# Two-layer hybrid encoder trunk: the two sequences as one token block, or as two streams half a layer apart

## The chip, the core and the metric

The kernel runs on one core of one Trainium2 chip. Its engines are TensorE (PE; PEld is its weight load), VectorE (DVE), ScalarE (ACT), GpSimd (POOL) and SyncE (SP), which issues nearly all DMAs. Each engine takes its instructions in a fixed order. The metric is the device time of one execution in microseconds, smaller being better.

## The reference, cut to what matters

A trunk of two layers runs over two independent sequences, a prompt of 512 tokens and a sample of 256, each with 16 learned meta tokens ahead: 528 and 272 tokens, 800 together. All weights are shared by both.

```python
for l in range(DEPTH):                                   # 2 layers, D = 1024
    proj = rms_norm(h, norm_mix[l]) @ w_in[l]            # 1024 x 2944
    xa, ga, xq, xi, xff, xfb, xg, xu = split(proj)
    ya = rglru_branch(xa, ga, ...)                       # 384 wide, scans in both directions
    yb = hgrn2_branch(xq, xi, xff, xfb, xg, ...)         # 384 wide, chunks of 64 tokens
    yc = s5_branch(xu, ...)                              # 256 wide, 16 groups of 16 with 64 complex states
    ym = concat([rms_norm(ya), rms_norm(yb), rms_norm(yc)]) * mix_gain[l]
    h = h + ym @ w_out[l]                                # 1024 x 1024
    h = h + relu(rms_norm(h, norm_mlp[l]) @ w_up[l])**2 @ w_down[l]   # 4096 wide
return rms_norm(h[:, N_META:], norm_final)
y_prompt, y_sample = _trunk(x_prompt, ...), _trunk(x_sample, ...)
```

## The kernel before

Features lie on partitions and the 800 tokens of both sequences along the free dimension. A product (`product`, L426) multiplies blocks of 128 x 128 weights with two halves of 400 tokens each and gathers over k in one PSUM bank; there are three such banks ("mm"). Weights and operands are float32, split exactly into a float32r high part and a low part, and three passes are made: high by high (L434), high weight by low operand (L435), low weight by high operand (L436). In layer 1 the meta tokens fall away after the mixers: w_out runs over 512 + 256 tokens there and the MLP over 384 + 384.

A block of weights is 128 columns of 1024 rows, 512 KB. `fetch` (L441) issues its DMA into one of three buffers "wr"; `wsplit` (L416) makes the high part with a ScalarE copy (L419) and the low part with a GpSimd subtraction (L420), two buffers each. Each weight is read once. An activation's result u in the MLP is split in the same way (L1128 ScalarE, L1129 GpSimd); relu and square are L1123 and L1124, and w_down's products are added to the residual by L1150.

The mixers of a layer (`mix`, L985) are issued as steps by a hand-written list per layer, `ORDERS`: `hi`/`hc`/`gh`/`hf` are the projections, chain, gate and end of an HGRN tile (chain `hgrn`, L597 to L694), `ri`/`rc` an RG-LRU tile, `si`/`sc`/`sf` the S5 projection, scan (`s5`, L879, eight groups per 128 features with table loads "E", "F", "TB", "W") and gated end. `PR` moves some steps in priority, `TG`, `NB` and `MO` say where they take their SBUF, and `KS` which outputs stay on chip; the others go to DRAM (`keep`, L1019) and come back (`finish`, L1001). `fA`, `fB`, `fC` normalise a group and split it into w_out's operands. `mix_out` (L1066) runs w_out in three passes in layer 0 and two in layer 1, a pass for the groups that are done (`LT`); a late group is scaled by the tokens' 1/rms after its product (L1098, L1099). The S5 tables (a step size, decays, their powers) are made by `s5_setup` (L706 to L872), whose DVE arithmetic is L726 to L731: for layer 0 at the start, for layer 1 within the first MLP, behind a mark in its first w_down. The order on each engine follows from issue order and priorities.

Of the kernel before, what the change touches and what calls it, by code (L numbers as in the profile page):

```python
# [30 lines left out]
SEQ = ((0, 528), (528, 272))
T = 800
EPS = 1e-6
NCH = 100
XA, GA, XQ, XI, XFF, XFB, XG, XU = 0, 384, 768, 1152, 1536, 1920, 2304, 2688
CH = [16 + 64 * n for n in range(8)] + [544 + 64 * n for n in range(4)]
# [38 lines left out]

class Trunk:
    def __init__(self, ctx, tc, ins, outs):
# [1157 lines left out]
```

## Time and profile before

| | |
|---|---|
| median of 3 runs (lowest, highest) | 2200.86 us (2199.04, 2205.67) |
| the profiled execution, its span | 2201.6 us (the page gives no other time of it) |
| busy: PE, DVE, ACT, POOL | 2087.4, 1118.9, 753.8, 811.9 us |
| instructions of PE, DVE, ACT, POOL | 14,082, 2,258, 1,141, 622 |
| DMA | 160.74 MB, 73 GB/s on average |
| queue of SP's DMAs, share of 16 engines' span | 23.8% |

Busy time is a sum over the span; an engine that is busy for 37% can still set the end of a stage. The stages of the span are, in order: start, setup and layer-0 mixers (to about 565 us), layer-0 w_out and MLP (to 1165), layer-1 mixers with w_out (to 1635), layer-1 MLP (to 2185), and the store-out. A row of the trace gives an instruction's start and duration, its engine, line and operands and, in brackets, how long the engine had been idle before it and what ended that.

### The profile page before, as it was taken

To read this page: it belongs to the slowest core of one execution; us is meant where nothing else is said; L and a number is where in the kernel's file an instruction comes from. 1 tells how busy PE (TensorE), PEld (TensorE's weight loads), DVE (VectorE), ACT (ScalarE), POOL (GpSimd) and SP (SyncE) were. 2 spreads that over 40 slices of the span, in tenths; PEclk is the share of its full clock that TensorE was granted. 3 is DMA by queue.
4 is the path that set the end of the run, shared out by engine and by line. 5 is a ranking of instruction groups with operands and counts; after the bars stand their busy time and mean duration, and the time that the engine had idled before them with its cause. 6 is when DMAs were issued, how large, how long until landed. Compare 5 with 4: busy or idle time off the path is not lost.

```text
span 2201.6 us, 34495 instructions
## 1 busy us (share of the span) xinstructions
PE 2087.4 (95%) x14082; PEld 1957.7 (89%) x14082; DVE 1118.9 (51%) x2258; ACT 753.8 (34%) x1141; POOL 811.9 (37%) x622
## 2 busy tenths in 40 slices
PE   8899899889989899999999999998998999999998
PEld 6889897677979899999998879886888999999997
DVE  6884748487657871221155855746368221112224
ACT  6233535454322232212225553436432122222222
POOL 1672112263433443333444213322434343434343
PEclk9899899899999999999999999998999999999998
DMA  5322111342211431122122113221321112122221
GB/s 182 96 81 76 38 40 56 101 129 57 68 48 58 109 119 58 58 64 61 58 95 78 57 37 97 74 59 48 113 79 58 58 58 68 59 67 65 60 67 68
DMA packets 230886, 160.74 MB, mean 73 GB/s; under 512 B 33270, under 2 KB 217784, under 8 KB 230728
## 3 DMA queue, kind: packets, MB, share of 16 engines
q1 hardware_dynamic: 229832, 156.95, 23.8%
q8 instruction: 111, 1.82, 0.4%
q10 hardware_dynamic: 896, 1.58, 0.2%
q14 instruction: 47, 0.39, 0.1%
HBM read 131.32 MB, written 27.18 MB: 72 GB/s over the span
## 4 chain that ended last, share of the span: by engine, by line
PE 60%; DVE 10%; ACT 2%; issue 1%; POOL 1%; DMA 1%; SPq 0%; DVEq 0%; POOLq 0%; ACTq 0%
PE mm L435 18%; PE mm L434 18%; PE mm L436 18%; PE hb L664 2%; PE hb L582 1%; DVE m L1163 1%; DVE h L1172 1%; PE rb L510 1%; DVE xl L379 1%; DVE m L1164 1%; DVE h L1154 1%; DVE r L1173 0%; DVE m L1124 0%; PE rb L862 0%; POOL wl L420 0%
## 5 line engine op out<-in xcount | busy, mean ns | idle before, releaser
L420 POOL TENSOR_TENSOR wl<-wr,wh 128x1024 fp32r<-128x1024 f32 (+3 forms) x214 | 479.3, 2240 | 1005.5 <-ACT wh L419 982.7
L434 PE MATMUL mm<-xh,wh 128*128 128x400 f32 (+3 forms) x2016 | 710.2, 354 | 33.1 <-DVE m L1124 11.1
L435 PE MATMUL mm<-xl,wh 128*128 128x400 f32 (+3 forms) x2016 | 713.9, 355 | 6.0 <-POOL xl L383 2.9
L436 PE MATMUL mm<-xh,wl 128*128 128x400 f32 (+3 forms) x2016 | 701.1, 349 | 0.7 <-POOL wl L420 0.5
L419 ACT ACTIVATE wh<-wr 128x1024 fp32r<-128x1024 f32 (+3 forms) x214 | 205.7, 962 | 764.9 <-PE mm L435 658.5
L434 PEld LDWEIGHTS mm<-xh,wh 128*128 128x128 f32 x2016 | 388.6, 193 | 52.7 <-DVE m L1124 14.1
L435 PEld LDWEIGHTS mm<-xl,wh 128*128 128x128 f32 x2016 | 389.1, 193 | 18.5 <-DVE xl L379 4.1
L436 PEld LDWEIGHTS mm<-xh,wl 128*128 128x128 f32 x2016 | 388.8, 193 | 8.9 <-POOL wl L420 0.9
L434 PE MATMUL mm<-u,wh 128*128 128x400 f32 (+1 forms) x1024 | 349.1, 341 | 6.2 <-DVE m L1124 6.2
L435 PE MATMUL mm<-u,wh 128*128 128x400 f32 (+1 forms) x1024 | 349.6, 341 | 0.0
L436 PE MATMUL mm<-u,wl 128*128 128x400 f32 (+1 forms) x1024 | 348.3, 340 | 0.0
L1150 DVE TENSOR_TENSOR h<-mm,h 128x400 f32<-128x400 f32 (+1 forms) x256 | 144.5, 565 | 331.2 <-PE mm L436 331.2
L1124 DVE TENSOR_TENSOR m<-m,mm 128x400 f32<-128x400 f32 (+1 forms) x128 | 71.1, 559 | 369.2 <-ACT m L1123 369.2
L434 PEld LDWEIGHTS mm<-u,wh 128*128 128x128 f32 x1024 | 193.3, 189 | 7.8 <-DVE m L1124 7.1
L435 PEld LDWEIGHTS mm<-u,wh 128*128 128x128 f32 x1024 | 193.2, 189 | 0.1
L436 PEld LDWEIGHTS mm<-u,wl 128*128 128x128 f32 x1024 | 193.1, 189 | 0.1
L1129 POOL TENSOR_TENSOR u<-m,u 128x800 fp32r<-128x800 f32 (+1 forms) x64 | 127.3, 1990 | 53.5 <-ACT u L1128 45.4
L1123 ACT ACTIVATE m<-mm 128x400 f32<-128x400 f32 (+1 forms) x128 | 62.3, 489 | 129.9 <-PE mm L436 115.8
L582 PE MATMUL hb<-hs,hs 64*64 64x64 f32 x2016 | 85.7, 236 | 8.8 <-ACT hs L615 5.6
L582 PEld LDWEIGHTS hb<-hs,hs 64*64 64x64 f32 x2016 | 72.2, 146 | 24.5 <-issue 11.4
L1128 ACT ACTIVATE u<-m 128x800 fp32r<-128x800 f32 (+1 forms) x64 | 55.1, 861 | 83.1 <-DVE m L1124 73.2
L616 DVE TENSOR_TENSOR hd<-hd,hd 128x800 f32<-128x800 f32 (+2 forms) x48 | 43.1, 902 | 13.3 <-ACT hs L614 12.8
(365 smaller groups left out, 2245.8 us busy)
## 6 DMA issues: line engine op xcount, KB each, us to landing
wr<-in_w_up_dram SPq DMA_DIRECT2D x64, 512.0 KB
wr<-in_w_down_dram SPq DMA_DIRECT2D x64, 512.0 KB
wr<-in_w_in_dram SPq DMA_DIRECT2D x46, 512.0 KB
h<-h SPq DMA_DIRECT2D x16, 400.0 KB
wr<-in_w_out_dram SPq DMA_DIRECT2D x32, 192.0 KB
TB<-t SPq DMA_DIRECT2D x24, 200.0 KB
F<-t SPq DMA_DIRECT2D x16, 256.0 KB
E<-t SPq DMA_DIRECT2D x16, 256.0 KB
```

What stands on the lines that cost most here:

```text
L419: self.nc.scalar.activation(hi[:], raw, AF.Copy)
L420: self.nc.gpsimd.tensor_tensor(out=lo[:], in0=raw, in1=hi[:].bitcast(F32), op=SUB)
L434: nc.tensor.matmul(ps[:, 0:n], wh, xh[:, c0 : c0 + n], start=(k == 0), stop=False)
L435: nc.tensor.matmul(ps[:, 0:n], wh, xl[:, c0 : c0 + n], start=False, stop=False)
L436: nc.tensor.matmul(ps[:, 0:n], wl, xh[:, c0 : c0 + n], start=False, stop=(k == last))
L582: nc.tensor.matmul(ps[c % 2 * 64 : c % 2 * 64 + 64, c // 2 * 64 : c // 2 * 64 + 64], K[hr, c0 : c0 + 64], Q[hr, c0 : c0 + 64], start=True, ...
L664: mm = lambda out, w, x: nc.tensor.matmul(out, w, x, start=False, stop=False, skip_group_check=True)
L1123: nc.scalar.activation(t[:, sl], ps, AF.Relu)
L1124: nc.vector.tensor_tensor(out=t[:, sl], in0=t[:, sl], in1=ps, op=MULT)
L1128: nc.scalar.activation(u[:, 0], t[:], AF.Copy)
L1129: nc.gpsimd.tensor_tensor(out=u[:, 1], in0=t[:], in1=u[:, 0].bitcast(F32), op=SUB)
L1150: mark = nc.vector.tensor_tensor(out=t[:, sl], in0=ps, in1=t[:, sl], op=ADD)
```

## The change

The class `Trunk` becomes a class `Shared` (constants, parameters, PSUM) and two `Stream`s, a for the prompt (528 tokens, pieces of 272 and 256) and b for the sample (272 tokens, one piece), each with its own SBUF side, its own residual and weight buffers (three wr, two wh and wl each). Each stream reads and splits all weights for itself. In layer 1, w_out and the MLP run over 256 + 256 and 256 tokens. `ORDERS`, `PR`, `TG`, `KS`, `LT` give way to one list for both layers and streams; every mixer output goes to DRAM and returns in `finish`, which scales it ahead of the split; w_out is one pass over eight k tiles after `fC`. S5 uses 66 and 34 chunks of 8 tokens, its scan reads the decay from a column (`r8`) in place of a table. The setup of layer 1 is issued between b's first `feed` and b's second mixers, in a's SBUF.

```diff
-SEQ = ((0, 528), (528, 272))
-ORDERS = [
-    "hi0 hc0 ri0 gr0 hi1 si0 rc0 gr2 hc1 ri1 gh1 hi2 rc1 sc0 hc2 si1 ri2 hf1 hf2 hf0 rc2 fB fA sc1 sf fC",
-    "ri0 rc0 hi0 hc0 ri1 rc1 ri2 rc2 si0 sc0 si1 sc1 sf gh2 hi1 hc1 hi2 gh1 hc2 gr0 hf2 hf0 fA hf1 fC fB",
-]
-HALVES = ((0, 400, 0), (400, 400, 400))
-HALVES_LAST = ((16, 512, 0), (544, 256, 512))
+ORDER = "hi0 hc0 ri0 rc0 gh0 hf0 hi1 hc1 ri1 rc1 gh1 hf1 hi2 hc2 ri2 rc2 gh2 hf2 si0 sc0 si1 sc1 sf fA fB fC"
...
-        def keep(k, y):
-            if k in last:
-                got["y", k] = y
-            else:
-                nc.sync.dma_start(self.ydr[k][:], y[:])
+        keep = lambda k, y: nc.sync.dma_start(self.ydr[k][:], y[:])
...
+        for m in range(KD):
+            raw = self.raw((128, KD, 128))
+            nc.sync.dma_start(raw[:], src[:, :, m * 128 : m * 128 + 128])
+            hi, lo = self.wsplit(raw[:])
+            t, res = self.t("h", (128, n)), self.s((128, n))
+            nc.sync.dma_start(res[:], self.hdr[m][:, self.T - n : self.T])
...
-            if b == 0 and l + 1 < L:
-                with self.using("t", "rb"), self.tc.issue_after(mark.ins):
-                    self.s5_setup(l + 1)
...
+        with a.phase("s0", dict(p=(10752, 1), t=(576, 11)), "t", "rb"):
+            a.setup()
+            a.buffers()
+            b.buffers()
+            with b.phase("i", dict(x=(D, 3), m=(D, 2), h=(b.T, 8)), "m", "rb"):
+                b.load(a)
+            a.s5_setup(0)
+        b.mixers(0, **MIX_B)
+        with a.phase("i", dict(x=(D, 5), m=(D, 1), h=(a.T, 8)), "m", "rb"):
+            a.load(None)
+        a.mixers(0, **MIX_A)
+        b.feed(0, h=8, m=3, u=6)
+        with a.phase("s1", dict(p=(10752, 1), t=(576, 11)), "t", "rb"):
+            a.s5_setup(1)
+        b.mixers(1, **MIX_B)
+        a.feed(0, h=8, m=3, u=6)
+        a.mixers(1, **MIX_A)
+        b.feed(1, h=8, m=3, u=6, t=6)
+        a.feed(1, h=8, m=3, u=6, t=9)
```

`feed` is `mix_out`, `mlp` and the next layer's norm. In the changed kernel the product's passes are L431 to L433, the weight split L416 and L417, the S5 steps L876 to L931 (DVE L896, L897, L906 to L909), relu and square L1052 and L1053, the setup's complex products L700 to L705.

The first place is TensorE's order in layer 0 of the kernel before, while the second half of the S5 runs. Products into "mm" (w_out's first pass, k tile after k tile) stand around the S5 matmuls of a group (L913 input side, L943 output side).

```order
L435 MATMUL mm_787_5143<-xl2_657_4531,wh_783_5126 128x400
L436 MATMUL mm_787_5143<-xh2_656_4530,wl_784_5127 128x400
L434 MATMUL mm_792_5162<-xh0_652_4522,wh_790_5158 128x400
L435 MATMUL mm_792_5162<-xl0_653_4523,wh_790_5158 128x400
L913 MATMUL hb_702_4752<-hs_697_4739 64x100 x8
L434 MATMUL mm_794_5175<-xh0_652_4522,wh_790_5158 128x400
L943 MATMUL hb_695_4723<-hs_689_4683,hs_694_4708 100x128 x4
L943 MATMUL hb_696_4731<-hs_689_4683,hs_694_4708 100x128 x4
L436 MATMUL mm_792_5162<-xh0_652_4522,wl_791_5159 128x400
```

The same place after the change, stream a's S5 in layer 0 (66 chunks): transposes L876, input L893, output L920 and L923.

```order
L923 MATMUL rb_6690<-rs_6651,rs_6677 66x128
L923 MATMUL rb_6698<-rs_6651,rs_6677 66x128
L876 MATMUL rb_6712<-ident_81,rs_6629 128x66 x2
L893 MATMUL rb_6722<-su_6708,rs_6709 64x66 x8
L920 MATMUL rb_6749<-rs_6706,su_6708 66x128
L920 MATMUL rb_6757<-rs_6706,su_6708 66x128
L923 MATMUL rb_6749<-rs_6710,rs_6736 66x128
```

What moved: the products that stood between the S5 matmuls are gone from this stretch (rows 2602 to 2660 of TensorE's order hold none); b's w_out and first w_up blocks stand before it, in the first half of the same S5, and the rest of b's MLP behind it.

The second place is DVE's order. Before, in the layer-0 MLP, where the setup of layer 1 (L726 to L731, tiles t) goes between evacuations of w_up (L1124, from PSUM bank mm):

```order
L726 TENSOR_TENSOR t_1007_6425<-t_1007_6425 128x16
L727 TENSOR_TENSOR t_1007_6425<-t_1007_6425 128x16
L728 TENSOR_TENSOR t_1007_6425<-t_1007_6425 128x16
L1124 TENSOR_TENSOR m_1111_7142<-m_1111_7142,mm_1112_7143 128x400
L730 TENSOR_TENSOR t_1007_6425<-t_1007_6425 128x16
L731 TENSOR_TENSOR t_1007_6425<-t_1007_6425 128x16
```

After, the third evacuation of b's w_up (L1053), row 1014 of DVE's order, with stream a's S5 (L896 to L908) behind it:

```order
L1053 TENSOR_TENSOR m_7436<-m_7436,mm_7437 128x272
L466 SCALAR_TENSOR_TENSOR rs_6552<-rs_6565,rs_6552 128x528
L896 TENSOR_TENSOR rs_6661<-rb_6663,rs_6648 128x264
L897 TENSOR_TENSOR rs_6662<-rb_6663,rs_6648 128x264
L906 SCALAR_TENSOR_TENSOR rs_6676<-r_22_136,rs_6661 128x66 x4
```

And the fourth, row 1307, among the setup of layer 1 (L700 to L705):

```order
L700 TENSOR_TENSOR t_10031<-t_10028,t_9761 128x32
L701 TENSOR_TENSOR t_10031<-t_10027,t_9761 128x32
L704 TENSOR_TENSOR t_9978<-t_9978,t_9982 128x4x2
L1053 TENSOR_TENSOR m_7473<-m_7473,mm_7474 128x272
L705 TENSOR_TENSOR t_9979<-t_9979,t_9982 128x4x2
```

What moved: before, an evacuation stands after some 30 setup instructions all through the setup; now 261 setup instructions and the rest of stream a's S5 and ends stand between the third and the fourth.

## Rows read from the trace of the kernel before

**Rows 1.** The page, busy time of each engine, and the granted clock in 40 slices.

```profile
PE 2087.4 (95%) x14082; PEld 1957.7 (89%) x14082; DVE 1118.9 (51%) x2258; ACT 753.8 (34%) x1141; POOL 811.9 (37%) x622
...
PEclk9899899899999999999999999998999999999998
```

**Rows 2.** Busy time by stretch: window, us, five engines busy, PEclk, DMA share, GB/s.

```profile
0.00:270.00 270.00, 243.01 (x1919) 217.75 (x1920) 200.42 (x589) 116.92 (x193) 112.55 (x132) 0.93 0.33 96
...
565.00:1165.00 600.00, 581.82 (x3164) 573.27 (x3163) 276.30 (x639) 145.32 (x204) 240.45 (x111) 0.98 0.24 73
...
1635.00:2185.00 550.00, 540.96 (x3086) 538.51 (x3085) 159.77 (x236) 127.61 (x166) 221.53 (x100) 0.99 0.20 59
2185.00:2202.00 17.00, 6.39 (x37) 5.70 (x37) 4.56 (x9) 6.12 (x9) 0.00 (x0) 0.59 0.51 186
700.00:750.00 50.00, 41.28 (x200) 39.81 (x199) 48.59 (x216) 8.68 (x12) 21.75 (x17) 0.86 0.39 98
```

**Rows 3.** The page's groups: the high-by-high pass, features and MLP operands.

```profile
L434 PE MATMUL mm<-xh,wh 128*128 128x400 f32 (+3 forms) x2016 | 710.2, 354 | 33.1 <-DVE m L1124 11.1
...
L434 PE MATMUL mm<-u,wh 128*128 128x400 f32 (+1 forms) x1024 | 349.1, 341 | 6.2 <-DVE m L1124 6.2
```

**Rows 4.** Timeline of TensorE, product streams (start us, us, line, operands, columns).

```profile
800.31 0.34 PE L436 MATMUL mm<-xh,wl 128*128 128x400 f32 x1
...
803.04 0.35 PE L436 MATMUL mm<-xh,wl 128*128 128x400 f32 x1
...
1702.52 0.34 PE L436 MATMUL mm<-xh,wl 128*128 128x384 f32 x1
...
1703.04 0.34 PE L436 MATMUL mm<-xh,wl 128*128 128x384 f32 x1
...
1601.90 0.28 PE L435 MATMUL mm<-xl,wh 128*128 128x256 f32 x1
...
1603.45 0.28 PE L436 MATMUL mm<-xh,wl 128*128 128x256 f32 x1
...
1565.79 0.41 PE L435 MATMUL mm<-xl,wh 128*128 128x256 f32 x1
...
1566.43 0.41 PE L435 MATMUL mm<-xl,wh 128*128 128x256 f32 x1
```

**Rows 5.** Splits in the layer-1 MLP by line: count, ns minimum/median/maximum, first and last start.

```profile
L420 POOL TENSOR_TENSOR wl<-wr,wh x36: 2388/2403/2407, 1805.3 to 2098.4; 128x1024 fp32r<-128x1024 f32 x36
...
L419 ACT ACTIVATE wh<-wr x36: 1060/1061/1063, 1804.1 to 2097.3; 128x1024 fp32r<-128x1024 f32 x36
...
L1129 POOL TENSOR_TENSOR u<-m,u x17: 1835/1843/1845, 1824.4 to 2092.3; 128x768 fp32r<-128x768 f32 x17
```

**Rows 6.** Timeline of DVE: start and end of one HGRN tile's chain, layer 1.

```profile
1386.61 1.83 DVE L609 TENSOR_TENSOR hd<-hd,hs 128x1600 f32<-128x1600 f32 x1
...
1472.17 0.99 DVE L693 TENSOR_TENSOR hs<-hs,hs 128x800 f32<-128x800 f32 x1 [5.22 <-ACT hs L413]
```

**Rows 7.** Timeline of DVE: the same step of two successive S5 groups, layer 0.

```profile
483.19 0.57 DVE L915 TENSOR_TENSOR hs<-hb,hs 128x400 f32<-128x400 f32 x1 [1.64 <-POOL hs L935]
...
494.19 0.56 DVE L915 TENSOR_TENSOR hs<-hb,hs 128x400 f32<-128x400 f32 x1
```

**Rows 8.** Timeline: a weight split on POOL, DVE beside it and afterwards.

```profile
798.96 2.40 POOL L420 TENSOR_TENSOR wl<-wr,wh 128x1024 fp32r<-128x1024 f32 x1 [6.94 <-ACT wh L419]
...
799.79 1.89 DVE L728 TENSOR_TENSOR t<-t,t 128x288 f32<-128x288 f32 x1
...
803.69 0.44 DVE L731 TENSOR_TENSOR t<-t,t 128x288 f32<-128x288 f32 x1
```

**Rows 9.** Timeline: a mixer output's store, and first use after its load, layer 1.

```profile
1575.38 0.34 SPq L1019 DMA_DIRECT2D y<-hs  x1
...
1583.03 0.97 ACT L378 ACTIVATE xh<-hs,pc 128x800 fp32r<-128x800 f32 x1 [5.86 <-DMA hs<-y]
```

**Rows 10.** Waits of SP: total us, times, longest, for stores of mixer outputs.

```profile
SPq L1019 <- DVE hs L1046: 21.8, 5, 7.4
```

More of the change, by code (lines that the diff above doesn't have):

```diff
@@ L30 @@
 DIN = 2944
[L31 to L32 removed]
 EPS = 1e-6
[L34 removed]
+NTB = 66
 XA, GA, XQ, XI, XFF, XFB, XG, XU = 0, 384, 768, 1152, 1536, 1920, 2304, 2688
[L36 removed]
 TWO_PI = 2 * math.pi
@@ L284, in load @@
             nc.sync.dma_start(xs[-1][0][:], a)
-            if len(xs) == 4:
+            if len(xs) == 3:
                 self.fetch("w_in", 0, XFF)
-        with self.using("t", "rb"):
-            self.columns(2, [("norm_mix", "l (k p) -> (l k) p")], nc.scalar)
+        if first:
+            first.columns(2, [("norm_mix", "l (k p) -> (l k) p")], nc.scalar)
         gain = self.pc["norm_mix"]
@@ new lines, in hgrn @@
+            prev = None
+            for k in range(n) if d == 0 else range(n - 1, -1, -1):
+                sl = SB[:, d, k]
+                par, at = col[k]
+                new = pss[par][:, at : at + 64]
+                if prev is None:
+                    nc.vector.tensor_copy(sl, new)
+                else:
+                    c = k - (1 - d)
+                    nc.vector.scalar_tensor_tensor(out=sl, in0=prev, scalar=tot[:, d, c : c + 1], in1=new, op0=MULT, op1=ADD)
+                prev = sl
@@ L685, in hgrn @@
+        nc.scalar.activation(O[:, META:T], ps[:, 0 : 64 * n], AF.Copy)
+        nc.scalar.activation(O[:, 0:META], pm[:, mo : mo + META], AF.Copy)
         q = self.s()
         nc.scalar.activation(q[:], O[:], AF.Square)
-        pss = []
-        for b in range(2):
-            ps = self.ps()
-            nc.tensor.matmul(ps[:, 0:400], self.bones[:], q[:, b * 400 : b * 400 + 400], start=True, stop=True)
-            pss.append(ps[:, 0:400])
-        rs = self.rstd(pss, 1.0 / 64, "eps")
+        rs = self.rstd(self.total(q, self.halves, self.bones), 1.0 / 64, "eps")
@@ L946, in s5 @@
-            z = self.s()
-            for b in range(2):
-                ps = self.ps()
-                for j in range(4):
-                    nc.tensor.transpose(ps[:, j * 100 : j * 100 + 100], flat(ZT[b][:, j]), self.ident[0:100, 0:100])
-                nc.scalar.activation(ap(z, b * 4, [[1, 4], [8, 100]]), ps[:, 0:400].rearrange("p (j c) -> p j c", j=4), AF.Copy)
-            self.gelu(z)
+                        nc.tensor.matmul(out, GH[1][r, d, ri], f[d][r, ri], start=False, stop=(d == 1 and ri == 1))
@@ L1060, in mix, with finish @@
-        for w in order:
-            off = PR[l].get(w, 0)
-            self.tc.cur_priority += off
-            step(w)
-            self.tc.cur_priority -= off
+        def finish(k0, nk):
+            ys = []
+            for k in range(k0, k0 + nk):
+                ys.append(self.s())
+                nc.sync.dma_start(ys[-1][:], self.ydr[k][:])
+            r = self.rstd(self.sumsq(ys), 1.0 / (128 * nk), "eps4" if k0 == 3 else "eps16")
+            for k, y in enumerate(ys, k0):
+                self.x[k] = self.split(k, y, self.pc["mix_gain"][:, l * KD + k : l * KD + k + 1], r)
@@ L1066, in mix_out @@
+        for w in ORDER.split():
+            tag = "hs" if w[0] == "h" or w in ("gh0", "gh1", "gh2", "fB") else "ss" if w[0] == "s" and "ss" in self.tags else "rs"
+            with self.using(tag, "hb" if tag == "hs" else "rb"):
+                if w[0] == "f":
+                    finish(*dict(fA=(0, 3), fB=(3, 3), fC=(6, 2))[w])
+                else:
+                    step(w[:2], int(w[2:] or 0))
     def mix_out(self, l):
         nc = self.nc
-        n, halves = (T, HALVES) if l < L - 1 else (768, HALVES_LAST)
@@ new lines, in mix_out, with ev @@
+        for m in range(KD):
[4 more added lines that the diff above has]
+            nc.sync.dma_start(res[:], self.hdr[m][:, self.T - n : self.T])
+            def ev(b, ps, t=t, res=res):
+                c0, w, o = halves[b]
+                nc.vector.tensor_tensor(out=t[:, o : o + w], in0=ps, in1=res[:, o : o + w], op=ADD)
+            self.product([(hi[:, k], lo[:, k]) for k in range(KD)], self.x, halves, ev)
+            new.append(t)
@@ L1106, in mlp @@
         n = h[0].shape[1]
-        halves = HALVES if n == T else ((0, 384, 0), (384, 384, 384))
+        halves = self.halves if n == self.T else tuple((o, w, o) for _, w, o in self.halves_last)
         self.x = [self.split(k, h[k], self.pc["norm_mlp"][:, l * KD + k : l * KD + k + 1], n=n) for k in range(KD)]
@@ new lines, in mixers, with feed @@
+    def mixers(self, l, **k):
+        U = self.T + 3
+        with self.phase(f"m{l}", {t: (dict(gw=512, hm=128, hn=32, su=2 * self.NCH, hd=2 * self.T).get(t, U), n) for t, n in k.items()}, "rs", "rb"):
+            self.mix(l)
+    def feed(self, l, **k):
+        with self.phase(f"f{l}", {t: (dict(u=2 * self.T, t=512).get(t, self.T), n) for t, n in k.items()}, "m", "rb"):
+            h = self.mlp(l, self.mix_out(l))
+            if l + 1 < L:
+                self.norm_in(l + 1, h)
+MIX_A = dict(gw=2, hm=3, hn=4, su=2, hd=5, hs=9, rs=13)
```

723 lines of the change are left out of this document (309 added, 414 removed).

## The prediction

> **What bounds the kernel now.** I read the busy times first [rows 1]: TensorE (PE) works 2087.4 of 2201.6 us and its granted clock is near full all along; the next engine, VectorE (DVE), has half as much. So time is TensorE's work plus the little that it waits, and a stage is slow where its DVE share is high. The table by stage [rows 2] shows it: in the first 270 us DVE is busy for 200.42 us and TensorE idles for 27; in the layer-0 MLP (565 to 1165 us) TensorE works 581.82 of 600 us, in the layer-1 MLP 540.96 of 550. Idle time is 114 us altogether, so the change can win at most that much if it adds no work. The profiled execution (2201.6 us) lies 0.7 us over the median of the runs, 2200.86; the sum below is made against the former, and the difference is ignored.
>
> **The products get shorter, and more of them.** A weight tile of 128 x 128 is used in three passes, which makes 4,560 uses in all (per layer 552 for w_in, 192 for w_out, 768 for w_up, 768 for w_down). Two token halves make 9,120 matmuls now; [rows 3] are two of the groups, six of which make them up. The change has three pieces per pass (272 and 256 columns of the prompt, 272 of the sample), so 13,680. The pace is read from start to start in full streams [rows 4]: at 400 columns 803.04 - 800.31 over 15 steps, 182 ns; at 384 columns 0.52 over 3, 173; at 256 columns 1.55 over 13, 119. For 272 I interpolate: 119 + 16 x (182 - 119)/144 = 126. Per tile and pass 400 + 400 costs 364 ns, 272 + 256 + 272 costs 371: 7.6 ns more with unrounded paces, for 2,832 of those uses (layer 0, and w_in of layer 1). In the layer-1 MLP 384 + 384 becomes 3 x 256: 357 - 346, so 11.6 ns, for 1,536. The 192 of layer-1 w_out (512 + 256 before) I put between, at 8.6. Sum 21.5 + 17.8 + 1.7 = **41 us** of TensorE, all on the path. The Trainium skill, page "TensorE: Matmul & The Clock Gate", section "Back-to-back issue gap", gives an isolated matmul its columns at the full clock and 2.5 ns: 4,560 more would cost 11 us and the forecast would fall by 30; the 182 ns at 400 columns, where that gap would be 169, speak against it here, and the measured paces are taken.
>
> With 24 matmuls to a weight block of 512 KB, the sample (B) uses a block in 24 x 126 ns = 3.03 us (2.86 in layer 1's MLP), the prompt (A) in 24 x 245 = 5.89 (5.72). Without any idle time TensorE would need 2087.4 + 41 = 2128 us, which is a floor.
>
> **The weights are read and split twice.** A split is a ScalarE copy of 1.06 us and a GpSimd subtraction of 2.40 [rows 5]. At 5.89 us per block both hide. At 3.03 they nearly don't: with two buffers, a pair of blocks costs copy, subtraction and one block's matmuls less their start under the end of the split, (1.06 + 2.40 + 3.03 - 0.25)/2 = 3.12 us per block. GpSimd also subtracts the split of u, one of 1.84 us at 768 columns, so 0.65 at 272, per w_up block: 0.33 per block on average. Bounds are 3.03 (all hidden) and 3.8 (copy, subtraction and 0.33 in series); I take 3.12. In the layer-0 MLP the rate of bytes doubles to 172 GB/s; the store-out at the end moved 186 GB/s [rows 2], so it is possible.
>
> **Two streams need two sets of dependent chains.** An HGRN tile's chain of 800 tokens runs 1386.61 to 1472.17 plus 0.99, 86.6 us [rows 6]. The chain of A has 66% of the tokens: 57 if all scales, 86.6 if nothing does; I take 70, the middle, since its many short instructions do not shrink. B (34%): 29 to 86.6, I take 50, nearer the low end since most elementwise work is DVE's. An S5 group of 800 tokens follows the last after 11.0 us [rows 7]; for A 7.3 to 11, taken 9, for B 3.7 to 11, taken 7. In the layer-0 mixers before, w_out's first passes stand between S5 groups (first order fence); now w_out waits for all three groups, and the other stream must give the cover. The second fence says that in A's second S5 half it doesn't: group follows group, no product between. The DVE fences say why: of B's first w_up block only three evacuations have been issued when A's S5 rows come, and the fourth stands behind A's S5 and the second S5 setup (some 261 instructions); three PSUM banks are then full.
>
> Setup on DVE: 216 instructions in 48.59 us (stretch 700 to 750 us) [rows 2], 0.225 each, 59 us for 261; bounds 0 (all beside A's S5) and 88 (1.5 times, by the locked instructions of [rows 8]); I take 59, as nothing else stands between the two evacuations.
>
> **The path, stage by stage (us, running total).**
> - Start to A's first products: DVE has 624 instructions before B's first S5 one: 360 of setup at 0.225 (81) and 264 of the mean 0.34 of the first 270 us (90), 171 at its share of 74% [rows 2] is 230; B's S5, 8 groups x 7 = 56: **286**.
> - A's layer-0 mixers: four blocks before the first chain 24, three chains 210: 520. A's S5 without products 8 x 9 = 72: 592. Setup 59: 651.
> - B's layer-0 w_out and MLP: 72 blocks, of which 14 lie beside A's S5; 58 x 3.12 = 181: 832.
> - Norm 4, B's layer-1 mixers 12 + 3 x 50: 998.
> - A's w_out and MLP, 72 x 5.89 = 424: 1422. A's layer-1 mixers 234: 1656, its S5 72: 1728.
> - B's last MLP 58 x 3.04 = 176: 1904. A's, alone, 72 x 5.72 = 412: 2316. Norm 4 and the tail 17, as now (the last stretch) [rows 2]: 2337, rounded to **2340**.
>
> *Mixer outputs through DRAM.* A store and load takes 1575.38 to 1583.03, 7.7 us [rows 9]. All but the last pair per stream and layer return early; those four would cost 31 us if bare; A's S5 end and B's products stand beside, so I take 0 (ends 0 and 31). SP issues in order, so a store that waits for its data holds the other stream's weights: five such stores held it 21.8 us, 4.4 each, 7.4 at most [rows 10]. There are 32 stores for 9: 23 x 4.4 = 101 as upper end; two blocks in the other buffers cover 6.1 us of products, so 0. *Fewer w_out passes* remove 48 evacuations and 48 additions on DVE, no matmul; DVE is not the limit there: 0. *No decay table*: the scan reads a broadcast column, fewer DMA bytes, 0. *A's load* lies behind B's mixers and only its first operands are awaited: within the start's term.
>
> **The rivals.**
> *R1, the streams do cover each other, not slower.* The order is a queue, not a clock: if B's w_out and w_up fill A's S5 stretches, the 72 + 59 + 72 go: 2340 - 203 = 2137, near the floor. For it: B's blocks are in the list beside A's S5. Against: evacuation four's place behind the setup, a fixed order. It decides from 140 us covered on. 6%.
> *R2, weight supply and split bind B.* At 3.8 us per block, 116 blocks cost 79 more: 2420. For it: GpSimd's 3.05 us of work per w_up block exceed the 3.03 of its matmuls. Against: w_down blocks carry no u. 10%.
> *R3, GpSimd locks out DVE in the mixers.* A DVE multiply of 0.44 us took 1.89 beside a 2.40 us subtraction that was first [rows 8], 1.45 lost. 62 more splits (46 of w_in, 16 of w_out) fall into mixers where DVE sets the end: 90 us, 2430. It decides if the chains, rather than the products, set A's mixer stages. 12%. The Trainium skill, page "SBUF — State Buffer", section "Who interferes with whom", has the rule: a DVE instruction with two SBUF inputs and a GpSimd instruction that reads SBUF exclude each other, the first one holding the port; the trace agrees with it in those 1.89 us.
> The forecast itself, in-order stalls as summed: 72%.
>
> **How the numbers follow.** Ends about the sum: A's chains (6) -77 and +100, B's (3) -62 and +110, setup -59 and +29, splits -10 and +79, S5 of A -27 and +32, of B -26 and +32, trips +31, SP +101. They will not all fall together; as root of the squares 121 below, 206 above. Where TensorE is left thin its clock falls: at the lower level a 256-column matmul takes 213 ns, not 119 (at 1565 us) [rows 4], which lies within the upper ends. Nine tenths below and seven tenths above: **2230 to 2490**. That takes in R2 and R3 and leaves out R1 and the far tail, 20% together. A measurement tells 0.3%, about 7 us, from no change. Faster 0.05 (R1, most of it), same 0.02, slower 0.93.
>
> **What would show it.** Right: TensorE busy above 2128 us by little but idle by some 200; matmuls x13,680 at 0.126 us pace; gaps of TensorE in A's S5 stretches ended by DVE evacuations (L1053) or S5 steps; B's MLP blocks at about 3.1 us, waiting on L416 or L417; A's last MLP alone in about 412 us. Wrong: B's blocks between A's S5 groups with no gaps (R1); B's blocks at 3.8 (R2); DVE durations in A's mixers of over twice their size without GpSimd (R3); or a start much longer than 286 us.

## The result, and the profile after

The changed kernel takes 2680.13 us (median of 4 runs, 2674.31 to 2683.45) against 2203.27: ratio 1.2146, 95% interval 1.2094 to 1.2199. Slower was right; the time lies 190 us over the upper end of the range.

The page of the changed kernel: busy times, and in 40 slices TensorE, GpSimd and the granted clock.

```profile
PE 2307.5 (86%) x19414; PEld 2132.4 (80%) x19414; DVE 1218.0 (45%) x2973; ACT 1102.3 (41%) x2018; POOL 1305.4 (49%) x1009
...
PE   6776689997559988899699999999866999899998
...
POOL 3672222225368873343354555322635885455454
PEclk8877588998679997899799999999977999899999
```

Against [rows 1] TensorE is busy for 220 us more and idle for 258 more; GpSimd has 1305 us of work in place of 812. TensorE's digits sink in four places: the start (slices 1 to 5), slices 10 to 12, 20, and 30 to 31. The granted clock sinks at each of them.

By stretch (columns as in [rows 2]), cut where a stage of a stream begins:

```profile
0.00:364.00 364.00, 243.92 (x1790) 191.30 (x1791) 216.84 (x721) 171.29 (x409) 156.18 (x229) 0.71 0.38 110
364.00:608.00 244.00, 232.52 (x2441) 214.91 (x2440) 153.99 (x290) 129.43 (x209) 69.43 (x39) 0.95 0.21 61
608.00:772.00 164.00, 94.46 (x654) 79.82 (x654) 97.74 (x395) 59.49 (x119) 80.17 (x101) 0.71 0.41 115
772.00:967.00 195.00, 186.13 (x1388) 177.82 (x1388) 56.70 (x114) 84.08 (x123) 157.62 (x88) 0.99 0.51 154
967.00:1147.00 180.00, 152.60 (x1269) 132.57 (x1269) 135.78 (x335) 96.28 (x208) 73.41 (x37) 0.83 0.38 113
1147.00:1661.00 514.00, 478.89 (x3886) 460.53 (x3885) 163.71 (x348) 164.30 (x320) 247.07 (x189) 0.95 0.31 96
1661.00:1905.00 244.00, 227.97 (x2440) 210.35 (x2438) 155.96 (x291) 131.41 (x212) 75.78 (x44) 0.97 0.24 70
1905.00:2050.00 145.00, 96.76 (x691) 80.81 (x690) 58.90 (x121) 59.72 (x120) 73.76 (x90) 0.74 0.40 121
2050.00:2237.00 187.00, 170.48 (x1371) 163.34 (x1371) 42.17 (x98) 76.78 (x111) 153.43 (x88) 1.00 0.48 147
2237.00:2665.00 428.00, 418.68 (x3474) 416.96 (x3473) 131.70 (x259) 126.06 (x186) 217.66 (x109) 0.98 0.30 90
```

Line by line beside the prediction's stages, in us:

| stage | summed | measured | miss |
|---|---|---|---|
| start to a's first products | 286 | 364 | +78 |
| a's layer-0 HGRN and RG-LRU | 234 | 244 | +10 |
| a's S5, second setup (14 blocks of b counted as hidden) | 131 | 164 | +33 |
| b's other blocks of w_out and MLP | 181 | 195 | +14 |
| norm and b's layer-1 mixers | 166 | 180 | +14 |
| a's w_out and MLP | 424 | 514 | +90 |
| a's layer-1 HGRN and RG-LRU | 234 | 244 | +10 |
| a's S5 | 72 | 145 | +73 |
| b's last MLP | 176 | 187 | +11 |
| a's last MLP | 412 | 428 | +16 |
| norm and end | 21 | 14 | -7 |

Where a's many products run (the second, sixth, seventh and last stage) TensorE is at 93% or more and the clock at 0.95 to 0.98. The largest misses are the start, a's two S5 stretches, and a's w_out and MLP, in which b's layer-1 S5 stands. In this last one TensorE was short of work for a part only:

```profile
1172.00:1250.00 78.00, 76.94 (x664) 70.45 (x663) 27.61 (x73) 31.25 (x91) 35.65 (x51) 1.00 0.46 135
```

I also cut TensorE's time in the traces from start to start: a product counts with its pace [rows 4], what it takes beyond that up to 2.2 times as excess (low clock and short waits), the rest as gap; other matmuls count up to 0.5 us each, the rest as gap. Before: products 1629 at pace, excess 79, gaps 65; other matmuls 378, gaps 38. After: 1669, 117, 126; 535, 222. So the pace gives 40 of 480 us, just as summed; excess gives 38, gaps 245, and 772 more small matmuls with slower ones 157. Of the 772, 672 are S5's: each stream runs all of its groups, and by the same count S5's matmuls take 145 us of TensorE for 60 and the gaps behind them 74 for 10.

### The profile page after: what moved, and what is told of

It reads as the page before. It is cut to its first block, busy times and chain, and to the rows that moved or that the text cites. A ratio compares the mean times of both kernels' runs of the same rounds, so it can differ in the third digit from the quotient of the medians.

```text
span 2679.2 us, 48559 instructions
## 1 busy us (share of the span) xinstructions
PE 2307.5 (86%) x19414; PEld 2132.4 (80%) x19414; DVE 1218.0 (45%) x2973; ACT 1102.3 (41%) x2018; POOL 1305.4 (49%) x1009
## 5 line engine op out<-in xcount | busy, mean ns | idle before, releaser
L417 POOL TENSOR_TENSOR wl<-wr,wh 128x1024 fp32r<-128x1024 f32 x380 | 945.3, 2489 | 895.4 <-ACT wh L416 847.4
L431 PE MATMUL mm<-xh,wh 128*128 128x272 f32 (+1 forms) x3024 | 905.1, 300 | 105.5 <-DVE m L1053 46.2
L433 PE MATMUL mm<-xh,wl 128*128 128x272 f32 (+1 forms) x3024 | 890.4, 296 | 9.2 <-POOL wl L417 9.1
L432 PE MATMUL mm<-xl,wh 128*128 128x272 f32 (+1 forms) x3024 | 892.7, 296 | 4.8 <-DVE xl L378 4.8
L416 ACT ACTIVATE wh<-wr 128x1024 fp32r<-128x1024 f32 x380 | 401.5, 1057 | 783.9 <-PE mm L432 570.9
L431 PEld LDWEIGHTS mm<-xh,wh 128*128 128x128 f32 x3024 | 599.6, 198 | 127.4 <-DVE m L1053 52.1
L433 PEld LDWEIGHTS mm<-xh,wl 128*128 128x128 f32 x3024 | 596.1, 198 | 17.7 <-POOL wl L417 14.9
L432 PEld LDWEIGHTS mm<-xl,wh 128*128 128x128 f32 x3024 | 599.6, 198 | 9.9 <-DVE xl L378 5.4
L431 PE MATMUL mm<-u,wh 128*128 128x256 f32 (+1 forms) x1536 | 435.7, 286 | 10.1 <-ACT wh L416 5.0
L432 PE MATMUL mm<-u,wh 128*128 128x256 f32 (+1 forms) x1536 | 433.2, 284 | 0.0
L433 PE MATMUL mm<-u,wl 128*128 128x256 f32 (+1 forms) x1536 | 428.4, 285 | 5.2 <-POOL wl L417 4.8
L431 PEld LDWEIGHTS mm<-u,wh 128*128 128x128 f32 x1536 | 288.4, 188 | 13.8 <-ACT wh L416 6.3
L1053 DVE TENSOR_TENSOR m<-m,mm 128x272 f32<-128x272 f32 (+1 forms) x192 | 80.6, 424 | 474.6 <-ACT m L1052 464.0
L433 PEld LDWEIGHTS mm<-u,wl 128*128 128x128 f32 x1536 | 285.8, 189 | 11.2 <-POOL wl L417 11.1
L1052 ACT ACTIVATE m<-mm 128x272 f32<-128x272 f32 (+1 forms) x192 | 72.1, 377 | 114.1 <-PE mm L433 82.5
```

The costliest lines, as they stand in the source:

```text
L416: self.nc.scalar.activation(hi[:], raw, AF.Copy)
L417: self.nc.gpsimd.tensor_tensor(out=lo[:], in0=raw, in1=hi[:].bitcast(F32), op=SUB)
L431: nc.tensor.matmul(ps[:, 0:n], wh, xh[:, c0 : c0 + n], start=(k == 0), stop=False)
L432: nc.tensor.matmul(ps[:, 0:n], wh, xl[:, c0 : c0 + n], start=False, stop=False)
L433: nc.tensor.matmul(ps[:, 0:n], wl, xh[:, c0 : c0 + n], start=False, stop=(k == last))
L1052: nc.scalar.activation(t[:, sl], ps, AF.Relu)
```

## The experiments

Two theories. **One, mine:** what costs is the streams' dependent work, S5 above all, in a fixed order without cover. **Two:** the doubled weights cost, either by supply or by GpSimd's splits (the prediction's R2 and R3). Differences are taken to the kernel before of the same session, or to the changed kernel's 2680.13.

### Parts of the change, one at a time, on the kernel before

**e1, three pieces.**

```diff
-HALVES = ((0, 400, 0), (400, 400, 400))
-HALVES_LAST = ((16, 512, 0), (544, 256, 512))
+HALVES = ((0, 272, 0), (272, 256, 272), (528, 272, 528))
+HALVES_LAST = ((16, 256, 0), (272, 256, 256), (544, 256, 512))
...
-        halves = HALVES if n == T else ((0, 384, 0), (384, 384, 384))
+        halves = HALVES if n == T else ((0, 256, 0), (256, 256, 256), (512, 256, 512))
```

> The kernel before, with every product in three pieces (272, 256, 272 tokens; 3 x 256 in layer 1) in place of two halves, and nothing else. My paces say 41 us more, 2244. A rival, that short pieces cost much more than their columns (evacuations, bank changes, more waits on three PSUM banks), wants over 100 more, 2300 and up.

2326.02 against 2207.28: 119 more (ratio 1.0531, 1.0508 to 1.0554). My paces gave 41, and fell. By stretch, cut where its stages end:

```profile
0.00:607.00 607.00, 535.60 (x4754) 475.41 (x4755) 396.93 (x968) 256.51 (x423) 212.05 (x261) 0.88 0.27 80
607.00:1221.00 614.00, 589.08 (x4696) 581.91 (x4695) 284.08 (x738) 151.38 (x237) 238.71 (x111) 0.98 0.24 72
1221.00:1740.00 519.00, 467.27 (x4542) 423.04 (x4541) 294.06 (x510) 218.20 (x336) 144.43 (x151) 0.90 0.22 63
1740.00:2310.00 570.00, 555.03 (x4620) 552.35 (x4618) 172.91 (x333) 132.79 (x198) 221.21 (x101) 0.99 0.19 57
```

The stages were 565, 600, 470 and 550 us; [rows 2] has the MLPs, and the mixers were:

```profile
0.00:565.00 565.00, 509.56 (x4008) 449.78 (x4009) 395.82 (x910) 256.00 (x424) 206.74 (x261) 0.93 0.29 86
...
1165.00:1635.00 470.00, 448.63 (x3792) 390.41 (x3791) 282.49 (x468) 218.77 (x338) 143.19 (x151) 0.96 0.24 70
```

The MLPs lose 14 and 20, about their pace; the mixers lose 42 and 49, though their 552 uses a layer cost 4 each by pace. **e13** keeps the pieces in w_out and the MLPs and takes them out of the mixers' projections:

```diff
+PIECES = ((0, 272, 0), (272, 256, 272), (528, 272, 528))
...
-        n, halves = (T, HALVES) if l < L - 1 else (768, HALVES_LAST)
+        n, halves = (T, PIECES) if l < L - 1 else (768, HALVES_LAST)
```

> The kernel before with three pieces in w_out and the MLP alone, the mixers' projections staying at two halves of 400. By the paces 3,456 uses take 1728 x 7.6 ns + 1536 x 11.6 ns + 192 x 8.6 ns = 33 us more, 2237. If short pieces are dear everywhere, most of the 119 comes here, 2290 and up; if the mixers' evacuations are what costs, 2230 to 2250.

2243.01, 41 more (1.0180, 1.0156 to 1.0204), near the 33. So 78 of the 119 come from the projections' pieces. The number of evacuations alone does not explain it: e1's mixers hold 968 and 510 VectorE instructions for 910 and 468, but e13's first 565 us hold 952 already, w_out's among them, and its first w_up evacuation starts no later than before (563.7 us for 569.2):

```profile
0.00:565.00 565.00, 507.35 (x4240) 450.94 (x4241) 399.40 (x952) 257.69 (x428) 211.68 (x262) 0.95 0.29 86
```

What is left is the projections' own few evacuations, 16 in layer 0 by these counts, or the order, which moves with the pieces; no run separates the two.

**e2, each weight block read and split twice.**

```diff
+            w = again() if b == 1 else w
...
-            self.product(self.fetch("w_in", l, c), self.x, HALVES, ev)
+            self.product(self.fetch("w_in", l, c), self.x, HALVES, ev, lambda: self.fetch("w_in", l, c, 1))
```

> The kernel before, with each weight block read and split a second time for the second half of the tokens. If the doubled weights are what costs (supply, split, GpSimd against VectorE), 200 us or more are added, 2400 and up. If what costs is the streams' own dependent work, a half block's matmuls (24 x 182 ns = 4.4 us) hide a split of about 3.1 us in the MLP, and only the mixers pay: 20 to 60 more, 2220 to 2260. The locked-port rival put 62 splits x 1.45 = 90 on it, 2290.

2374.30, 167 more (1.0748, 1.0730 to 1.0766): above my 20 to 60, below theory two's 200. Its first two stages:

```profile
0.00:619.00 619.00, 534.72 (x4000) 461.50 (x4001) 429.93 (x910) 289.24 (x470) 293.17 (x308) 0.88 0.36 105
619.00:1256.00 637.00, 591.04 (x3162) 574.75 (x3161) 306.43 (x638) 207.40 (x267) 400.99 (x174) 0.97 0.41 120
```

VectorE has 638 instructions in the MLP for the 639 of [rows 2], and is busy 306.43 us for 276.30: the same work takes longer while GpSimd's has grown from 240 to 401.

**e3, one w_out pass, all outputs through DRAM.**

```diff
-KS = [(2, 5, 6, 7), (2, 6, 7)]
-LT = [1, 2]
+KS = [(), ()]
+LT = [3, 3]
```

> The kernel before, with w_out in one pass after the last group and every mixer output through DRAM; order list and one token stream stay. If w_out's early passes are the cover of the S5 and HGRN chains, their loss shows: 16 blocks lose six of their eight k tiles beside the mixers in layer 0 and as many in layer 1, 288 matmuls x 0.182 = 52 us a layer at most, so 40 to 100 more, 2240 to 2300. If fewer passes are a gain for VectorE, it is the same or up to 20 less.

2266.88, 60 more (1.0245, 1.0211 to 1.0279), as cover lost would have it; the sum had put 0. The stage to the first MLP grows from 565 to 604, the layer-1 mixers from 470 to 492, the MLPs by 2 and 3. I could not tell the lost passes from the DRAM trips in it.

**e4, no S5 in the kernel before; e5, none in the changed one.** Same edit in both:

```diff
-                    got["z", i] = self.s5(l, i, got["s", i])
+                    got["z", i] = (self.gelu(got["s", i]), got["s", i])[1]
```

> The kernel before without the S5 scan of 32 groups: its gelu is taken of the projection itself, so the scan and its table loads are left out. S5's matmuls take 60 us of TensorE and 10 us of gaps stand behind them: 70 less if nothing else fills them, 2130. If S5's real price is in gaps elsewhere, more than 100 less.

> The changed kernel without the S5 scans (64 groups, both streams): gelu is taken of the projection itself, scans and table loads are left out. Theory: each stream runs all 16 groups of a layer, and TensorE's fixed order puts groups and products in series; S5 matmuls take 145 us and gaps of 74 us stand behind them, with the products' clock beside them some 30 more. So 220 to 270 less, 2410 to 2460, against 70 from the same cut in the kernel before. Rival (doubled weights are the cost): the stretches stay as long, since weights still have to be split, and under 120 go, 2560 and up.

2140.26, 67 less; and 2427.59, 253 less. Both as theory one had it: S5 costs the changed kernel 186 us more. Between the same marks e5 takes 71 us less in the start, 61 in a's first S5, 63 in a's layer-0 w_out and MLP, 56 after a's second HGRN and RG-LRU. The third is b's layer-1 S5, which no term of the sum held.

**e10, S5 twice in the kernel before.**

```diff
+                    self.s5(l, i, got["s", i])
                     got["z", i] = self.s5(l, i, got["s", i])
```

> The kernel before with every S5 scan made twice, the first result unused: 64 groups in place of 32, one token stream, the order list as it is. If a group costs what its removal gave (67 for 32), 2270. If what the changed kernel lost by S5 (253 against 67, so 186 more) is the number of groups with nothing to hide behind, 2350 to 2390.

2416.44, 211 more (1.0945, 1.0865 to 1.1025), somewhat above the higher forecast. Its mixers, with the MLPs unchanged at 600 and 550:

```profile
0.00:658.00 658.00, 567.66 (x4349) 493.95 (x4350) 428.64 (x977) 272.13 (x480) 235.87 (x341) 0.86 0.29 86
...
1258.00:1858.00 600.00, 528.18 (x4127) 451.85 (x4126) 320.59 (x535) 236.56 (x394) 169.99 (x231) 0.85 0.23 68
```

The first 32 groups cost 67 and the next 32 211. Of the 211, 138 are more busy time of TensorE in these two stages (509.56 and 448.63 us before), at a granted clock of 0.86 and 0.85 for 0.93 and 0.96; the rest is idle time. That the list's cover is spent once fits this, but no run shows it apart from the matmuls themselves.

**e9, the three parts together.** Its edits are those of e1 and e3, and e2's second read for the sample's piece (`b == 2`).

> The kernel before with three changes at once: three pieces, each weight block read and split again for the sample's piece, one w_out pass with all outputs through DRAM. One at a time they cost 119, 167 and 60. If each costs by itself, 346 more, 2550; if they wait for the same stretches of the mixers, 230 to 300, 2435 to 2505. What then is missing to 2680 is S5 done by each stream, the second setup's place and the streams' order.

2635.43, 430 more (1.1951, 1.1902 to 1.1999), more than the 346 of its parts and above both forecasts. But it is no copy of the changed kernel: its MLP stages are 717 and 648 us where 600 and 550 were; the changed kernel has no such loss in a's MLP. My guess, which no run tests, is that short and long pieces share the two split buffers. The run shows that the parts are big enough, not that they fall in the same place.

### Parts of the changed kernel

**e7, stream b without the low part's subtraction.**

```diff
+        if self.name == "b":
+            self.nc.scalar.activation(hi[:], raw, AF.Copy)
+            return hi, hi
```

> The changed kernel in which stream b uses the high part of a weight also as its low part: the subtraction on GpSimd for b is left out, reads, copies and matmuls stay. If GpSimd's splits bound b's MLPs (3.29 us per block measured, 3.03 by the matmuls), 116 blocks x 0.26 = 30 go, and with the mixers' lock on VectorE perhaps 20 more: 30 to 50 less, 2630 to 2650. If doubled splits are the main cost, 150 or more go, 2530 or less. If weight reads bind b, under 10.

2506.68, 173 less, where theory one had 30 to 50 and theory two 150 or more. Four of its stages (start, b's first MLP, b's layer-1 mixers, b's last MLP):

```profile
0.00:302.00 302.00, 235.04 (x1796) 185.87 (x1797) 175.07 (x722) 165.08 (x406) 89.73 (x204) 0.73 0.47 133
...
684.00:860.00 176.00, 174.85 (x1377) 174.64 (x1378) 51.82 (x115) 83.02 (x124) 26.13 (x33) 0.99 0.57 170
860.00:1016.00 156.00, 139.57 (x1292) 122.60 (x1291) 105.35 (x335) 95.95 (x211) 5.95 (x13) 0.92 0.45 131
...
1900.00:2062.00 162.00, 161.45 (x1365) 161.25 (x1365) 43.68 (x102) 77.19 (x114) 23.29 (x32) 1.00 0.56 170
```

The start is 62 us shorter, b's layer-1 mixers 24, b's MLPs 19 and 25, a's S5 stretches 21 and 14; a's mixers and MLPs stay within 7, but a's own splits were left in. In the start VectorE's 722 instructions take 175.07 us where 721 took 216.84, in b's mixers 335 take 105.35 where 335 took 135.78. In b's MLPs TensorE is now idle for about 1 us each at 170 GB/s, so supply of weights was not the bound there: R2's half about reads falls. One HGRN step of VectorE in the start, of the changed kernel and (as L602) of e7:

```profile
L599 DVE TENSOR_TENSOR hd<-hd,hd x18: 404/428/2620, 56.1 to 196.9; 128x272 f32<-128x272 f32 x12, 128x256 f32<-128x256 f32 x6
```

```profile
L602 DVE TENSOR_TENSOR hd<-hd,hd x18: 402/423/853, 49.3 to 187.4; 128x272 f32<-128x272 f32 x12, 128x256 f32<-128x256 f32 x6
```

The median is the same; two of the 18 take 2330 and 2620 ns. The longer one stands beside a split that was first:

```profile
114.25 2.40 POOL L417 TENSOR_TENSOR wl<-wr,wh 128x1024 fp32r<-128x1024 f32 x1
...
114.32 2.62 DVE L599 TENSOR_TENSOR hd<-hd,hd 128x272 f32<-128x272 f32 x1 [4.23 <-ACT hs L597]
```

The Trainium skill, page "SBUF — State Buffer", section "Who interferes with whom", has a VectorE instruction with two SBUF inputs contend with a GpSimd instruction that reads SBUF. These two rows agree. This step is 4 of the 42 us that VectorE is busy longer in the start; the setup (L700 to L705) is 25, with 90.3 us for 65.0.

**e12, b's low parts on VectorE,** nothing left out.

```diff
-        self.nc.gpsimd.tensor_tensor(out=lo[:], in0=raw, in1=hi[:].bitcast(F32), op=SUB)
+        (self.nc.vector if self.name == "b" else self.nc.gpsimd).tensor_tensor(out=lo[:], in0=raw, in1=hi[:].bitcast(F32), op=SUB)
```

> The changed kernel with stream b's low weight parts made on VectorE in place of GpSimd; everything is computed. A subtraction of 800 columns takes VectorE 0.99 us, so 1024 some 1.27. Leaving them out gave 173. If GpSimd's length of 2.4 us and the lock on VectorE are the cost, the MLPs keep their gain and the mixers give back 46 x 1.27 = 58: 115 less, 2565. If in-order VectorE makes b's weights late behind S5 and setup steps, no gain or slower, 2680 and up.

2554.68, 125 less, 10 from the forecast. So the engine that splits is most of the cost, not the reading. Its VectorE is busy longer than the changed kernel's 1218.0 and TensorE idles less:

```profile
PE 2257.3 (89%) x19414; PEld 2102.1 (83%) x19414; DVE 1340.4 (53%) x3163; ACT 1094.1 (43%) x2014; POOL 873.9 (34%) x819
```

A split on GpSimd can hold the others in two ways: it locks VectorE, and GpSimd's own steps stand behind it in their fixed order. No run separates them. VectorE's busy time shows the first (42 us in the start, 30 in b's layer-1 mixers), the rows under e11 the second.

**e6, no second setup** (layer 1 takes layer 0's tables), **and e8, the setup in b's MLP:**

```diff
-        with a.phase("s1", dict(p=(10752, 1), t=(576, 11)), "t", "rb"):
-            a.s5_setup(1)
+        g.sdr[1] = g.sdr[0]
```

> The changed kernel with layer 1 using layer 0's S5 tables, the second setup left out. If VectorE's in-order setup holds b's fourth w_up evacuation, the 42 us between a's S5 and b's MLP go nearly all: 30 to 45 less, 2635 to 2650. If something else (b's residual, norm, weights) is late next, under 15 less.

```diff
+            if b == 0 and hook:
+                with self.tc.issue_after(mark[-1].ins):
+                    hook()
```

> The changed kernel with the second setup issued within b's first MLP, after its first w_down block (as the kernel before has it in its own MLP), in place of after b's feed. If the setup's place is what costs, 30 to 45 less, as without it. If VectorE's order is made from readiness and the setup slides before the evacuations all the same, no change.

e6: 2637.28, 43 less: the size of its forecast, but not the place. Two of its stages, a's S5 and b's layer-1 mixers:

```profile
604.00:754.00 150.00, 96.07 (x654) 81.49 (x654) 55.63 (x109) 55.40 (x112) 71.59 (x91) 0.73 0.38 111
...
950.00:1105.00 155.00, 133.67 (x1192) 118.58 (x1194) 95.31 (x231) 89.84 (x186) 62.79 (x38) 0.88 0.34 98
```

They were 164 and 180 us, so a's S5 gives 14 and b's mixers 25: VectorE's 335 instructions there are 231 without the setup, a part of which runs beside b's chains. TensorE's longest wait of the changed kernel in 605 to 772 us (total, times, longest):

```profile
PE mm L431 <- DVE m L1053: 21.1, 3, 16.7
```

In e6 it is still 15.8 us in that window, in 5 pieces of at most 9.0, so most of that wait was not the setup's.

e8: 2710.78, 31 more; both its forecasts were wrong. TensorE waits for w_up's evacuation (L1054 there) 46.4 us in all, in 16 pieces of at most 9.0, for 47.5 in 13 of at most 16.7; without any setup, in e6, it is 40.2. a's S5 and b's layer-1 mixers come down to 147 and 150 us, but b's MLP, where the setup now stands, goes from 195 to 263:

```profile
755.00:1018.00 263.00, 217.18 (x1488) 203.66 (x1488) 180.80 (x509) 93.43 (x153) 175.73 (x98) 0.90 0.49 140
```

So the setup is not free in any of these places, and is dearest there.

**e11, b's two layers and then a's:**

```diff
         b.mixers(0, **MIX_B)
-        with a.phase("i", dict(x=(D, 5), m=(D, 1), h=(a.T, 8)), "m", "rb"):
-            a.load(None)
-        a.mixers(0, **MIX_A)
         b.feed(0, h=8, m=3, u=6)
...
         b.mixers(1, **MIX_B)
+        b.feed(1, h=8, m=3, u=6, t=6)
+        with a.phase("i", dict(x=(D, 5), m=(D, 1), h=(a.T, 8)), "m", "rb"):
+            a.load(None)
+        a.mixers(0, **MIX_A)
         a.feed(0, h=8, m=3, u=6)
         a.mixers(1, **MIX_A)
-        b.feed(1, h=8, m=3, u=6, t=6)
```

> The changed kernel with stream b's two layers first and then stream a's two, in place of half a layer apart. If the offset gives cover (a's S5 beside b's w_out, b's S5 beside a's w_out and first w_up), its loss costs 50 to 150, 2730 to 2830. If the streams stand one after the other anyhow, within 30 of 2680.

2745.52 (1.2449, 1.2387 to 1.2510), 65 more. The offset by half a layer is worth something, a quarter of what S5 costs. Why so little, the S5 rows say: TensorE in a's first S5, the timeline of the changed kernel.

```profile
678.39 0.67 PE L920 MATMUL rb<-rs,su 128*66 128x128 f32 x2 [0.65 <-DMA rs<-W]
678.71 0.58 PE L433 MATMUL mm<-xh,wl 128*128 128x272 f32 x1
679.08 0.43 PE L431 MATMUL mm<-xh,wh 128*128 128x272 f32 x1
679.31 0.43 PE L432 MATMUL mm<-xl,wh 128*128 128x272 f32 x1
...
681.45 0.29 PE L433 MATMUL mm<-xh,wl 128*128 128x272 f32 x1
...
682.58 0.29 PE L433 MATMUL mm<-xh,wl 128*128 128x272 f32 x1
682.70 0.38 PE L920 MATMUL rb<-rs,su 128*66 128x128 f32 x2
686.63 1.28 PE L923 MATMUL rb<-rs,rs 64*66 64x128 f32 x16 [3.54 <-POOL rs L914]
...
691.15 1.15 PE L893 MATMUL rb<-su,rs 128*64 128x66 f32 x16 [2.35 <-DMA rs<-E]
```

A product of b stands in one lump of four microseconds between two halves of L920, and behind it TensorE waits 3.5 for GpSimd's rotation (L914). A group here is one step of the chain, two of the 16-feature groups, as in the sum's eight a layer. VectorE's first step of successive groups:

```profile
677.78 0.43 DVE L896 TENSOR_TENSOR rs<-rb,rs 128x264 f32<-128x264 f32 x1 [3.84 <-PE rb L893]
692.39 0.43 DVE L896 TENSOR_TENSOR rs<-rb,rs 128x264 f32<-128x264 f32 x1 [10.05 <-PE rb L893]
700.74 0.43 DVE L896 TENSOR_TENSOR rs<-rb,rs 128x264 f32<-128x264 f32 x1 [5.02 <-PE rb L893]
```

8.4 us a group without products, 14.6 with one lump. What comes late is not TensorE but GpSimd and SP:

```profile
681.91 0.43 DVE L909 TENSOR_TENSOR rs<-rs,rs 128x264 f32<-128x264 f32 x1
...
683.96 2.34 POOL L417 TENSOR_TENSOR wl<-wr,wh 128x1024 fp32r<-128x1024 f32 x1 [3.06 <-ACT wh L416]
686.26 1.16 POOL L914 TENSOR_TENSOR rs<-rs,rs 128x65 f32<-128x65 f32 x4
...
677.68 9.01 SPq L1067 DMA_DIRECT2D wr<-in_w_down_dram  x3
686.78 0.46 SPq L868 DMA_DIRECT2D rs<-E  x1
...
695.29 0.42 DVE L909 TENSOR_TENSOR rs<-rs,rs 128x264 f32<-128x264 f32 x1
...
695.86 1.16 POOL L914 TENSOR_TENSOR rs<-rs,rs 128x65 f32<-128x65 f32 x4 [1.59 <-DVE rs L909]
```

VectorE's step before the rotation ends at 682.34, but the split of b's next block is first in GpSimd's order and itself waits for its copy: the rotation starts 3.9 us later, and in the next group, without a split, 0.15 us later. b's weight loads stand ahead of the group's table E in SP's order, and TensorE waits 2.35 us for that table. These two make up most of the 6.2 us between 14.6 and 8.4. So a block of b lengthens the chain that it should hide in by its split and its load.

### A version to beat both

**e14, w_in's low parts of the kernel before on VectorE; e15, layer 0's alone; e16, w_out's as well** (all one-line choices of the engine in `wsplit`; e16's, beside e14's):

```diff
-                hi, lo = self.wsplit(raw[:])
+                hi, lo = self.wsplit(raw[:], nc.vector)
```

> The kernel before with the low parts of w_in made on VectorE. Its 46 splits cost VectorE 46 x 1.27 = 58 us and spare it up to 46 x 1.45 = 67 of lock; GpSimd gets 110 us free beside the S5 and HGRN steps. If GpSimd's splits are a cost in the mixers already, 10 to 40 less, 2165 to 2195. If VectorE, being the mixers' limit and in order, makes weights late, 10 to 40 more.

> The kernel before with the low parts of w_in made on VectorE in layer 0 alone. With all of w_in there, the layer-0 mixers ended 15 us sooner and the layer-1 mixers took 2 longer. If the locks in layer 0, where VectorE also makes the setup, are the cost, 12 to 20 less, 2183 to 2190. If that was chance of the order, within 6 of the kernel before.

> The kernel before with the low parts of w_in and of w_out made on VectorE in both layers. w_out's blocks in three and two passes add 40 smaller subtractions, 20 us of VectorE, beside the late S5 groups. If GpSimd, which each S5 group needs twice, is the late one there, 5 to 15 less again, 2175 to 2190; if VectorE is, 10 to 25 more than with w_in alone, 2205 to 2220.

e14: 2194.78, ratio 0.9983 (0.9962 to 1.0004), no difference that can be told. e15: 2218.22, 1.0083 (1.0055 to 1.0111), 0.8% slower where 12 to 20 us less or no change was expected: the layer-0 theory falls. e16: 2193.52, 0.9962 (0.9947 to 0.9977): 0.4% faster than the kernel before, the one version that beats both. As e15 was slower with less of the same edit, part of these differences must be the order that comes out, and I give no cause for the 0.4%.

## Why the prediction was wrong, step by step

The direction was right, the size was not: 137 us were forecast on 2203, 477 came.

- **Paces and counts of the products: right.** 1629 became 1669 us of products at pace; in a's last MLP 3474 matmuls, nearly all of 256 columns, are busy for 418.68 us, 120.5 ns each. The Trainium skill's isolated gap (page "TensorE: Matmul & The Clock Gate", section "Back-to-back issue gap") gives an estimate of 109 there; the row decides.
- **"Without any idle time TensorE would need 2087.4 + 41 = 2128 us": too low.** TensorE is busy for 2307.5 us. The sum counted the products alone and left out that S5's matmuls are made once per stream, 145 us for 60 by the count above.
- **"Sum 21.5 + 17.8 + 1.7 = 41 us of TensorE, all on the path": the pieces were mis-sized.** On the kernel before they cost 119 (e1), 78 of it by the projections in the mixers (e13), where I had counted their matmuls alone.
- **"I take 3.12" and R3's place: the largest miss.** The sum held 10 us for GpSimd's second splits, 116 blocks of 0.09; leaving b's out gave 173 (e7), moving them to VectorE 125 (e12). b's MLP ran at 195/58 = 3.36 us a block against 3.03 in e7. R3 had the mechanism, at 12% and 90 us, and made it hang on a's mixers; the runs show it in the start and in b's mixers, where VectorE's chain sets the stage, and in a's S5, where the splits stand ahead of GpSimd's own steps. What a's own splits cost a's HGRN stretches no run tests; TensorE works 93% and more of them.
- **Start 286: 78 short.** b's first S5 matmul (L893) starts at 272 us where the sum had 230, from the mean prices of the kernel before; in e7 it starts at 205. From there to a's first product 92 us pass where the sum had 56.
- **S5: under-counted by 53.** The sum had 56 + 72 + 72 = 200; e5 gave 253. The price of a group was right: 8.4 us for the 9 taken where no product stands between. But b's S5 of layer 1 was put at nothing, without a reason: it stands beside a's w_out, the stage with the miss of 90, and is worth 63 there. The cover is real for the waits, as TensorE works 76.94 of 78 us there, but S5's matmuls need TensorE too.
- **"58 x 3.12", 14 blocks "beside A's S5": wrong.** They stand in lumps within five of its eight groups, and their splits and loads lengthen those groups.
- **"Fewer w_out passes ... 0" and the DRAM trips at 0: wrong;** 60 for both together on the kernel before (e3).
- **Setup 59: near in size by luck,** 43 by e6. Between a's S5 and b's MLP, where the sum had all of it, it is 14; 25 fall in b's layer-1 mixers.
- **HGRN chains 70 and 50: right in size,** 244 for 234 and 180 for 166, but a's were TensorE's work, and b's 180 hold 25 of setup.

The misses of these experiments add up to 163 + 78 + 53 + 60 - 16 = 338, near the 342 of the table; as they were made on two kernels and overlap (e5 and e7 both shorten a's S5 stretches), that sum is a check on size, not a proof of each share. R1 is refuted as a whole: a's S5 stretches, where it put its gain, were not filled. R2's splits are part of e7, its reads are refuted.

## What to carry to other kernels

Two streams share every in-order queue, and not only TensorE's: here a block of one inside the other's dependent chain made a group 14.6 us for 8.4, as its split stood ahead of the chain's step on GpSimd and its load ahead of the chain's table on SP. Look at the order of the helper engines before counting on cover. Splitting a batch into streams repeats everything that has a fixed price per instruction (scans by group, weight splits, evacuations), and that price is to be read in the stage where it has no cover: S5 cost 67 us under a list made for it and 211 for the same again. When an elementwise job is doubled on GpSimd, ask first what VectorE does at that moment, and what waits behind it on GpSimd.

## What was not expected of the hardware

Beside GpSimd's splits the same VectorE instructions took 24% longer in the start (216.84 for 175.07 us) and 29% in b's layer-1 mixers (135.78 for 105.35), though GpSimd was busy less than half the time. And thin stretches are paid twice, as the granted clock is 0.71 in the start and 0.71 and 0.74 beside a's S5. The lump of b's products above, in two parts (columns as in [rows 2]):

```profile
678.70:681.30 2.60, 2.60 (x13) 2.60 (x12) 0.87 (x4) 0.00 (x0) 2.19 (x5) 0.50 0.68 214
681.30:682.70 1.40, 1.40 (x13) 1.40 (x12) 1.01 (x4) 0.00 (x0) 0.00 (x0) 1.00 0.96 332
```

In the first, at 0.50, the 1.2 GHz level, its 272-column products went at 230 ns (679.08 to 679.31); in the second, at 1.00, the 2.4 GHz level, at 126 (681.45 to 682.58, nine steps). Before the fall TensorE had waited for S5's tables (0.65 us ahead of the first L920); before the rise it had run the lump's first products without a break.
